# Seven products for one more pair of gate and up blocks, first loads from another queue, and a final norm in two halves

## The chip, the core and the metric

The kernel runs on one core of one Trainium2 chip. The core has TensorE (matmuls into PSUM), VectorE, ScalarE and GpSimd (elementwise work), and SyncE, which issues loads. The time is device time of one execution in microseconds, the median of the runs of a round; it does not include the host.

## The reference, cut to what matters

The model has two layers. Each does a half-weighted SwiGLU feed-forward, a mixer and another half-weighted feed-forward, each behind an RMS norm; the mixer is latent attention in the first layer and a chunked mLSTM in the second. A final RMS norm ends it. There are 512 tokens of width 1024, and the hidden width of a feed-forward is 2816. All is float32.

```python
def rmsnorm(x, g, eps=RMS_EPS):
    xf = x.astype(F32)
    y = xf * lax.rsqrt(jnp.mean(xf * xf, axis=-1, keepdims=True) + eps)
    return (y * g.astype(F32)).astype(x.dtype)

def swiglu(h, w_gate, w_up, w_down):
    return (jax.nn.silu(h @ w_gate) * (h @ w_up)) @ w_down

def reference(...):
    for layer in range(DEPTH):
        x = x + 0.5 * swiglu(rmsnorm(x, ffn_norm[layer, 0]), ...)
        h = rmsnorm(x, mix_norm[layer])
        ...
        x = x + y.astype(x.dtype)
        x = x + 0.5 * swiglu(rmsnorm(x, ffn_norm[layer, 1]), ...)
    return rmsnorm(x, final_norm)
```

## The kernel before

The activations stay in SBUF transposed: eight tiles of 128 features by 512 tokens. There are six phases: f0, a (attention), f1, f2, m (mLSTM), f3. Every float32 operand is split into a high part, rounded by ScalarE (L162, L206), and a low part, the difference, made by VectorE (L163, L207); a product is three matmuls, high by high, high by low, low by high.

A feed-forward has eleven pairs of 128-wide blocks of gate and up. The first NB = 2 pairs are plain (L411): two halves of 48 matmuls of 512 columns each, on inputs with the gain but without the norm's scale, which is applied afterwards. The other nine pairs are groups of seven (L433): gate and up, the two halves of the tokens and the two halves of the features form a 2 x 2 by 2 x 2 block product that is done with seven block products instead of eight, each of 24 matmuls of 256 columns, in the order 1, 6, 5, 7, 2, 3, 4. Their operands need the norm's scale rb beforehand. The statistics come after the first plain half (L423): small matmuls on TensorE (L273), a power on GpSimd (L281), and a spread back over the partitions (L286 to L297). Then normed_blocks (L363) makes the operands in twelve steps: blocks b11, b12, b22, b21 of normed inputs (L373), their differences (L391 to L393, L407) and seven splits. Each step is deferred until a given number of further weight chunks has been asked for (L426).

Weights come in chunks of 128 x 1024 (512 KB). A chunk is split AHEAD = 2 chunks before its use (L186), and the high and the low parts have three buffers each. For a group of seven, five chunks are loaded and two more are added onto loaded ones: the tiles named sum are loaded by SyncE (L122) and get a second block added by an accumulating load from GpSimd (L125), which waits for the first. Two further sums of weights are made by VectorE (L150). SyncE issues loads in order, and a load waits there until its buffer is free: three for raw chunks, and 31 in the arena, which also holds sums, operands and activations.

The first three pairs' results go to the plain part of the down projection; the other eight form two slabs, whose down projection is again done by seven products (L571), the last of them product 4 of four chunks. For the last feed-forward the squares for the final norm are accumulated there (L634 to L641), and finish (L1301) makes the scale of all 512 tokens and multiplies the eight tiles.

In the mLSTM the heads go in pairs (L1223): a pass of the loop makes queries or keys by a convolution (L959), gates, the mixing of two heads with their values (mix), and the decay weights of two heads (decay). In the last pass the first product of the output projection, out(0, 0), stands between decay(6) and the pending sums of squares (L1240 to L1245).

The order of the instructions of an engine is fixed when the program is built: a scheduler takes them by readiness as it expects it and otherwise by the order of the program. On the chip each engine then runs its own list in order.

Of the kernel before, what the change touches and what calls it, by code (L numbers as in the profile page):

```python
# [26 lines left out]
F32 = mybir.dt.float32  # L27
F32R = mybir.dt.float32r
# [3 lines left out]
ALU = mybir.AluOpType  # L32
# [8 lines left out]
H = 8  # L41
W = 1024
NU = NF // 2
NB = 2
DC = 3
ARENA = 31
LOADS = 4
AHEAD = 2
WARM = 36
EPS = 1e-6  # L50
# [14 lines left out]
class Trunk:  # L65
# [48 lines left out]
    def load_pieces(self):  # L114

        name, pieces, pool, plus = self.loads[len(self.loaded)]

        ap = self.row(*name)
        raw = self.duo(pool, F32) if pool else self.wp.tile([P, W], F32, name="raw", tag="raw")
        self.loaded.append(raw)  # L120
        for a, b in pieces:
            self.nc.sync.dma_start(out=raw[:, a:b], in_=ap[:, a:b])  # L122
            yield
        if plus:
            self.nc.gpsimd.dma_start(out=raw, in_=self.row(*plus), accum_op=ALU.add)  # L125
# [105 lines left out]
    def norm_begin(self, gcol):  # L231
        self.xg = [None] * ND
        self.gcol = gcol
        self.acc = self.small.tile([P, T], F32, name="acc", tag="acc", bufs=2)
        self.nacc = 0

    def norm_split(self, d):

# [1 line left out]
        self.split_to(self.xg[d], self.x[d], self.vec(self.gcol + d))  # L240

    def norm_square(self, d):
        self.square(self.acc, self.x[d], self.nacc == 0)
        self.nacc += 1

    def norm_tile(self, d):

# [4 lines left out]
    def norm_half(self, d, n):  # L252

        t = slice(n * T // 2, n * T // 2 + T // 2)
        if self.gcol is not None:
            if self.xg[d] is None:
                self.xg[d] = self.pair()
            self.split_to([a[:, t] for a in self.xg[d]], self.x[d][:, t], self.vec(self.gcol + d))
        self.square(self.acc[:, t], self.x[d][:, t], False)

    def square(self, acc, src, first):
        if first:
# [3 lines left out]
            self.nc.scalar.activation(sq, src, AF.Square)  # L266
            self.nc.vector.tensor_tensor(out=acc, in0=acc, in1=sq, op=ALU.add)

    def rstd(self, acc, n, times=None):

        st = self.ps2.tile([P, T], F32, name="st", tag="st")
        for q in range(NT):
            self.nc.tensor.matmul(st[:, q:q + 1], acc[:, q * P:(q + 1) * P], self.one, start=True, stop=True)  # L273
        ms = self.small.tile([P, NT], F32, name="ms", tag="ms")
        if times is not None:
            self.nc.vector.tensor_tensor(out=ms, in0=st[:, 0:NT], in1=times, op=ALU.mult)
            self.nc.vector.tensor_scalar(ms, ms, 1.0 / n, EPS, ALU.mult, ALU.add)
        else:
            self.nc.vector.tensor_scalar(ms, st[:, 0:NT], 1.0 / n, EPS, ALU.mult, ALU.add)
        r = self.small.tile([P, NT], F32, name="r", tag="r", bufs=6)  # L280
        self.nc.gpsimd.tensor_tensor(out=r, in0=ms, in1=self.mhalf[:, 0:NT], op=ALU.pow)  # L281
        return r

    def spread(self, r):

        hi = self.small.tile([P, NT], F32R, name="rh", tag="rh")  # L286
        lo = self.small.tile([P, NT], F32, name="rl", tag="rl")
        self.split_to((hi, lo), r)
        bc = self.ps2.tile([P, T], F32, name="bc", tag="st")
        for n, part in enumerate((hi.bitcast(F32), lo)):  # L290
            diag = self.tmp.tile([P, T], F32R, name="diag", tag="t")
            self.nc.vector.tensor_tensor(
                out=diag.rearrange("p (a b) -> p a b", a=NT),
                in0=self.ident[:, None, :].broadcast_to([P, NT, P]),
                in1=part[:, :, None].broadcast_to([P, NT, P]), op=ALU.mult)
            self.nc.tensor.matmul(bc, self.onesr, diag, start=n == 0, stop=n == 1)
        return bc  # L297

# [6 lines left out]
    def begin(self, gcol):  # L305
# [10 lines left out]
        for i in range(WARM):  # L316
            nc.tensor.matmul(idle[:, 0:P], warm, warm, start=True, stop=True)
        self.par = self.const.tile([P, V_END], F32, name="par")
        nc.gpsimd.dma_start(out=self.par, in_=self.t["vecs"])
        cst = self.const.tile([P, self.t["cst"].shape[1]], F32, name="cst")  # L320
        nc.gpsimd.dma_start(out=cst, in_=self.t["cst"])
        self.ident = cst[:, 0:P]
# [88 lines left out]
    def plain(self, f, j, half, xg, outs):  # L411

        nc = self.nc
        g, u = self.bank("g"), self.bank("u")
        for k0 in range(0, ND, 4):
            w = self.weights("wgc", f, j, half, k0 // 4)
            for k in range(4):
                for b, o in ((g, 0), (u, P)):
                    self.mm3(b, w(k * 256 + o), xg[k0 + k], k0 + k == 0, k0 + k == ND - 1)
        if j + half == 0:  # L420
            if f == 0:
                self.constants()
            _, self.rb = self.stats()  # L423
            steps = self.normed_blocks(self.rb)
            for i in range(12):
                self.defer(1 + i // 2, lambda: next(steps))  # L426
        gr, ur = self.t512("gr"), self.t512("ur")
        nc.vector.tensor_tensor(out=gr, in0=g, in1=self.rb, op=ALU.mult)
        nc.vector.tensor_tensor(out=ur, in0=u, in1=self.rb, op=ALU.mult)
        nc.scalar.activation(gr, gr, AF.Silu)  # L430
        nc.vector.tensor_tensor(out=outs, in0=gr, in1=ur, op=ALU.mult)
# [139 lines left out]
    def down_seven(self, slabs):  # L571
# [57 lines left out]
        for c in range(4):  # L629
            product(bw, 7, c, last=False)  # L630
            product(bx, 2, c)
        add(1, 1, bw, -0.5)
        add(0, 0, bx, 0.5)
        for d in range(4):  # L634
            self.norm_tile(d)
        for c in range(4):
            product(bw, 4, c, first=False)
            self.norm_half(4 + c, 1)
        add(1, 0, bw, -0.5)
        for d in range(4, 8):  # L640
            self.norm_half(d, 0)  # L641

    def plan_ffn(self, f):
        for j in range(NB):
# [302 lines left out]
    def mlstm(self, next_gain):  # L947
# [258 lines left out]
        def out(part, i):  # L1206
            self.mix_out("wo2", part, i, ys)
# [15 lines left out]
        for p in range(3):  # L1223
            a, b = 2 * p, 2 * p + 1
            conv(p + 5)
            gate(a + 2)
            pending = [mix(a), mix(b)]
            if p == 1:
                steps = factors(0, pending)
                for i in (1, 2, 4):  # L1230
                    self.defer(i, lambda: next(steps))
                values(1)
                for i in range(4):
                    gated(i)
# [75 lines left out]
    def run(self, phases):  # L1310
        gains = {"f0": V_FFN, "f1": V_FFN + ND, "f2": V_FFN + 2 * ND, "f3": V_FFN + 3 * ND,
# [12 lines left out]
        for p, q in zip(phases, phases[1:] + ["end"]):  # L1324
# [104 lines left out]
```

## Time and profile before

| | us |
|---|---|
| median of three runs | 1867.44 (1866.93 to 1869.98) |
| profiled execution, its own time | 1857.42 |
| its span, first to last instruction | 1855.7 |
| TensorE busy | 1811.5 (98%) |
| VectorE busy | 1463.2 (79%) |
| ScalarE busy | 934.9 (50%) |
| GpSimd busy | 131.3 (7%) |

The profile is of one execution, whose time lies 10.0 us under the median of the timed ones. Its mean granted TensorE clock is 0.992 of full speed. In the views PE is TensorE, DVE is VectorE, ACT is ScalarE, POOL is GpSimd, SP is SyncE; a q behind a name is the engine's sequencer, which issues. L with a number is a line of the kernel.

### The profile page before, as it was taken

The numbers are of one execution on the slowest core, as the hardware profiler recorded it, in microseconds if no ns is written. First come the engines' busy times: TensorE is split into PE (matmuls) and PEld (weight loads), VectorE is DVE, ScalarE is ACT, GpSimd is POOL, SyncE is SP. The second block draws the span as 40 slices with busy tenths as digits, with TensorE's granted clock in tenths as the row PEclk, the third lists the DMA queues.
The fourth block names the chain that finished last, engine by engine and source line by source line (L and its number), as shares of the span: only waits on it lengthen the run. The fifth ranks groups of instructions, "written<-read, shape, count | busy, mean of one in ns | idle before, by whom it ended". The sixth has DMA issues, their size and how long they took to land.

```text
span 1855.7 us, 30086 instructions
## 1 busy us (share of the span) xinstructions
PE 1811.5 (98%) x12240; PEld 1662.8 (90%) x12240; DVE 1463.2 (79%) x1931; ACT 934.9 (50%) x1339; POOL 131.3 (7%) x154
## 2 busy tenths in 40 slices
PE   9999999999999999999999999999998999999996
PEld 7999989978887999989989999997876779999896
DVE  7877899777767877877796878778877778788875
ACT  5444545567544444544544444455757544445442
POOL 0010011000000010000001000100000000100010
PEclk9999999999999999999999999999998999999998
DMA  6683567421124684566377456733221246845662
GB/s 205 177 236 110 162 187 163 137 74 63 46 73 150 159 243 128 140 181 153 126 219 205 133 162 187 175 105 101 80 69 57 69 126 181 236 125 149 184 159 91
DMA packets 74906, 265.66 MB, mean 143 GB/s; under 512 B 8336, under 2 KB 9360, under 8 KB 74768
## 3 DMA queue, kind: packets, MB, share of 16 engines
q1 hardware_dynamic: 57312, 200.30, 30.9%
q0 software_dynamic: 17456, 63.44, 19.4%
q8 instruction: 96, 1.57, 0.3%
q14 instruction: 42, 0.34, 0.1%
HBM read 261.62 MB, written 2.10 MB: 142 GB/s over the span
## 4 chain that ended last, share of the span: by engine, by line
PE 73%; issue 13%; DVE 8%; ACT 3%; DMA 2%; POOL 0%; POOLq 0%; DVEq 0%; ACTq 0%
PE pz L450 4%; PE pw L449 4%; PE pw L448 4%; PE pz L449 4%; PE pz L448 4%; PE pw L450 3%; PE y L194 3%; PE y L196 3%; PE y L195 3%; PE px L449 3%; PE px L448 3%; PE px L450 3%; PE py L450 2%; DMA raw<-in_wgs 2%; PE py L448 2%
## 5 line engine op out<-in xcount | busy, mean ns | idle before, releaser
L162 ACT CAST whi<-raw 128x1024 fp32r<-128x1024 f32 (+1 forms) x278 | 284.9, 1025 | 412.2 <-issue 131.1
L163 DVE TENSOR_TENSOR wlo<-raw,whi 128x1024 fp32r<-128x1024 f32 (+1 forms) x278 | 330.5, 1190 | 109.1 <-ACT whi L162 108.1
L162 ACT CAST whi<-sum 128x1024 fp32r<-128x1024 f32 x208 | 217.5, 1047 | 278.5 <-PE pz L449 80.8
L163 DVE TENSOR_TENSOR wlo<-sum,whi 128x1024 fp32r<-128x1024 f32 x208 | 252.8, 1221 | 72.0 <-ACT whi L162 72.0
L150 DVE TENSOR_TENSOR sum<-raw,sum 128x1024 f32<-128x1024 f32 x88 | 107.2, 1219 | 25.6 <-DMA raw<-in_wgs 25.1
L125 POOL DMA_DIRECT2D sum<-in_wgs x72 | 61.6, 855 | 640.2 <-DMA sum<-in_wgs 278.3
L450 PE MATMUL py<-b6h,wlo 128*128 128x256 f32 x288 | 83.5, 290 | 10.6 <-DVE wlo L163 10.5
L448 PE MATMUL py<-b6h,whi 128*128 128x256 f32 x288 | 82.8, 288 | 2.2 <-ACT whi L162 2.2
L449 PE MATMUL py<-b6l,whi 128*128 128x256 f32 x288 | 82.4, 286 | 0.0
L450 PE MATMUL pz<-b5h,wlo 128*128 128x256 f32 x288 | 81.5, 283 | 0.8 <-DVE wlo L163 0.8
L450 PE MATMUL pw<-b7h,wlo 128*128 128x256 f32 x288 | 81.2, 282 | 0.0
L450 PE MATMUL px<-b2h,wlo 128*128 128x256 f32 x288 | 81.2, 282 | 0.0
L450 PE MATMUL pz<-b3h,wlo 128*128 128x256 f32 x288 | 81.2, 282 | 0.0
L450 PE MATMUL pw<-b4h,wlo 128*128 128x256 f32 x288 | 81.2, 282 | 0.0
L449 PE MATMUL pw<-b7l,whi 128*128 128x256 f32 x288 | 81.2, 282 | 0.0
L449 PE MATMUL pz<-b3l,whi 128*128 128x256 f32 x288 | 81.2, 282 | 0.0
L449 PE MATMUL px<-b2l,whi 128*128 128x256 f32 x288 | 81.2, 282 | 0.0
L449 PE MATMUL pw<-b4l,whi 128*128 128x256 f32 x288 | 81.2, 282 | 0.0
L450 PE MATMUL px<-b1h,wlo 128*128 128x256 f32 x288 | 81.2, 282 | 0.0
L449 PE MATMUL px<-b1l,whi 128*128 128x256 f32 x288 | 81.2, 282 | 0.0
L449 PE MATMUL pz<-b5l,whi 128*128 128x256 f32 x288 | 81.2, 282 | 0.0
L448 PE MATMUL px<-b1h,whi 128*128 128x256 f32 x288 | 81.2, 282 | 0.0
(418 smaller groups left out, 6137.1 us busy)
## 6 DMA issues: line engine op xcount, KB each, us to landing
raw<-in_wgs SPq DMA_DIRECT2D x108, 512.0 KB, 4.7
sum<-in_wgs SPq DMA_DIRECT2D x72, 512.0 KB, 6.8
sum<-in_wgs POOLq DMA_DIRECT2D x72, 512.0 KB, 7.2
sum<-in_wds POOLq DMA_DIRECT2D x48, 512.0 KB, 6.0
raw<-in_wds SPq DMA_DIRECT2D x48, 512.0 KB, 3.3
sum<-in_wds SPq DMA_DIRECT2D x32, 512.0 KB, 4.5
raw<-in_wgc SPq DMA_DIRECT2D x30, 512.0 KB, 3.3
raw<-in_wdn SPq DMA_DIRECT2D x24, 512.0 KB, 4.0
```

What stands on the lines that cost most here:

```text
L125: self.nc.gpsimd.dma_start(out=raw, in_=self.row(*plus), accum_op=ALU.add)
L150: self.nc.vector.tensor_tensor(out=t, in0=a, in1=b, op=ALU.add)
L162: self.nc.scalar.copy(out=hi[:, a:b], in_=raw[:, a:b])
L163: self.nc.vector.tensor_tensor(out=lo[:, a:b], in0=raw[:, a:b], in1=hi[:, a:b].bitcast(F32), op=ALU.subtract)
L194: mm(out, lhs[0], rhs[0], start=start, stop=False)
L195: mm(out, lhs[0], rhs[1], start=False, stop=False)
L196: mm(out, lhs[1], rhs[0], start=False, stop=stop)
L448: mm(out, wh, bh[:, b], start=first and e + k == 0, stop=False, skip_group_check=True)
L449: mm(out, wh, bl[:, b], start=False, stop=False, skip_group_check=True)
L450: mm(out, wl, bh[:, b], start=False, stop=last and e + k == 4, skip_group_check=True)
```

## The change

NB becomes 1, so that a feed-forward has one plain pair and ten groups of seven. The twelve steps of normed_blocks get a list of their own, STEPS, of due times. The first load of a tile sum for gate and up goes to GpSimd's queue instead of SyncE's, ahead of the accumulating one. The load of the parameters at the start goes to SyncE's queue instead. In the mLSTM's last pass out(0, 0) is called before decay(6). The final norm is done for tokens 256 to 511 while product 4 of the last down projection is still to come, and for tokens 0 to 255 after it; for the second of these the squares of four tiles are summed by the statistics matmuls instead of VectorE, and the outputs are made by ScalarE with GpSimd for all eight tiles of the first half and for two of the other, and by VectorE for six.

```diff
@@ -41,10 +41,12 @@
 H = 8
 W = 1024
 NU = NF // 2
-NB = 2
+NB = 1
 DC = 3
 ARENA = 31
 LOADS = 4
+
+STEPS = 1, 1, 1, 1, 2, 2, 3, 4, 5, 5, 6, 7
 AHEAD = 2
 WARM = 36
 EPS = 1e-6
@@ -119,7 +121,8 @@
         raw = self.duo(pool, F32) if pool else self.wp.tile([P, W], F32, name="raw", tag="raw")
         self.loaded.append(raw)
         for a, b in pieces:
-            self.nc.sync.dma_start(out=raw[:, a:b], in_=ap[:, a:b])
+            queue = self.nc.gpsimd if plus and name[0] == "wgs" else self.nc.sync
+            queue.dma_start(out=raw[:, a:b], in_=ap[:, a:b])
             yield
         if plus:
             self.nc.gpsimd.dma_start(out=raw, in_=self.row(*plus), accum_op=ALU.add)
@@ -232,7 +235,7 @@
         self.xg = [None] * ND
         self.gcol = gcol
         self.acc = self.small.tile([P, T], F32, name="acc", tag="acc", bufs=2)
-        self.nacc = 0
+        self.nacc = [0, 0]
 
     def norm_split(self, d):
 
@@ -240,8 +243,8 @@
         self.split_to(self.xg[d], self.x[d], self.vec(self.gcol + d))
 
     def norm_square(self, d):
-        self.square(self.acc, self.x[d], self.nacc == 0)
-        self.nacc += 1
+        self.square(self.acc, self.x[d], self.nacc == [0, 0])
+        self.nacc = [n + 1 for n in self.nacc]
 
     def norm_tile(self, d):
 
@@ -256,7 +259,8 @@
             if self.xg[d] is None:
                 self.xg[d] = self.pair()
             self.split_to([a[:, t] for a in self.xg[d]], self.x[d][:, t], self.vec(self.gcol + d))
-        self.square(self.acc[:, t], self.x[d][:, t], False)
+        self.square(self.acc[:, t], self.x[d][:, t], self.nacc[n] == 0)
+        self.nacc[n] += 1
 
     def square(self, acc, src, first):
         if first:
@@ -266,33 +270,38 @@
-    def rstd(self, acc, n, times=None):
+    def rstd(self, acc, n, times=None, tiles=range(NT)):
...
+        accs = acc if isinstance(acc, list) else [acc]
+        for i, q in enumerate(tiles):
+            for k, a in enumerate(accs):
+                self.nc.tensor.matmul(st[:, i:i + 1], a[:, q * P:(q + 1) * P], self.one, start=k == 0,
+                                      stop=k == len(accs) - 1)
...
@@ -316,7 +325,7 @@
         for i in range(WARM):
             nc.tensor.matmul(idle[:, 0:P], warm, warm, start=True, stop=True)
         self.par = self.const.tile([P, V_END], F32, name="par")
-        nc.gpsimd.dma_start(out=self.par, in_=self.t["vecs"])
+        nc.sync.dma_start(out=self.par, in_=self.t["vecs"])
         cst = self.const.tile([P, self.t["cst"].shape[1]], F32, name="cst")
         nc.gpsimd.dma_start(out=cst, in_=self.t["cst"])
         self.ident = cst[:, 0:P]
@@ -422,8 +431,8 @@
                 self.constants()
             _, self.rb = self.stats()
             steps = self.normed_blocks(self.rb)
-            for i in range(12):
-                self.defer(1 + i // 2, lambda: next(steps))
+            for i in STEPS:
+                self.defer(i, lambda: next(steps))
         gr, ur = self.t512("gr"), self.t512("ur")
         nc.vector.tensor_tensor(out=gr, in0=g, in1=self.rb, op=ALU.mult)
         nc.vector.tensor_tensor(out=ur, in0=u, in1=self.rb, op=ALU.mult)
@@ -630,15 +639,23 @@
             product(bw, 7, c, last=False)
             product(bx, 2, c)
         add(1, 1, bw, -0.5)
+        if self.gcol is None:
+            for d in range(8):
+                self.norm_half(d, 1)
+            self.finish(1)
         add(0, 0, bx, 0.5)
         for d in range(4):
-            self.norm_tile(d)
+            self.norm_half(d, 0) if self.gcol is None else self.norm_tile(d)
         for c in range(4):
             product(bw, 4, c, first=False)
-            self.norm_half(4 + c, 1)
+            if self.gcol is not None:
+                self.norm_half(4 + c, 1)
         add(1, 0, bw, -0.5)
-        for d in range(4, 8):
-            self.norm_half(d, 0)
+        if self.gcol is None:
+            self.finish(0)
+        else:
+            for d in range(4, 8):
+                self.norm_half(d, 0)
 
     def plan_ffn(self, f):
         for j in range(NB):
@@ -1237,9 +1254,12 @@
             if p == 0:
                 for f in pending:
                     f()
+            if p == 2:
+                out(0, 0)
             decay(a + 2)
-            conv(p + 2) if p < 2 else out(0, 0)
-            if p == 2:
+            if p < 2:
+                conv(p + 2)
+            else:
                 for f in pending:
                     f()
             decay(b + 2)
@@ -1298,14 +1318,29 @@
             self.plan(("wo2", i // 4, i % 4))
 
 
-    def finish(self):
+    def finish(self, n):
+
+
         nc = self.nc
-        rb = self.spread(self.rstd(self.acc, D))
+        t = slice(n * T // 2, n * T // 2 + T // 2)
+        accs = [self.acc]
+        if n == 0:
+            for d in range(4, 8):
+                accs.append(self.t512("sq"))
+                nc.scalar.activation(accs[-1][:, t], self.x[d][:, t], AF.Square)
+        bc = self.spread(self.rstd(accs, D, tiles=range(2 * n, 2 * n + 2)))
+        rb = self.small.tile([P, T], F32, name="rb", tag="rb", bufs=2)[:, :T // 2]
+        nc.scalar.copy(out=rb, in_=bc)
         for d in range(ND):
-            o = self.t512("o")
-            nc.vector.scalar_tensor_tensor(out=o, in0=self.x[d], scalar=self.vec(V_FIN + d), in1=rb,
-                                           op0=ALU.mult, op1=ALU.mult)
-            nc.sync.dma_start(out=self.out[d * P:(d + 1) * P, :], in_=o)
+            o = self.t512("o")[:, :T // 2]
+            gain = self.vec(V_FIN + d)
+            if n or d % 3 == 2:
+                nc.scalar.activation(o, self.x[d][:, t], AF.Identity, scale=gain)
+                nc.gpsimd.tensor_tensor(out=o, in0=o, in1=rb, op=ALU.mult)
+            else:
+                nc.vector.scalar_tensor_tensor(out=o, in0=self.x[d][:, t], scalar=gain, in1=bc,
+                                               op0=ALU.mult, op1=ALU.mult)
+            nc.sync.dma_start(out=self.out[d * P:(d + 1) * P, t], in_=o)
 
     def run(self, phases):
         gains = {"f0": V_FFN, "f1": V_FFN + ND, "f2": V_FFN + 2 * ND, "f3": V_FFN + 3 * ND,
@@ -1328,7 +1363,6 @@
                 self.mla(gains[q])
             else:
                 self.mlstm(gains[q])
-        self.finish()
```

## Rows read from the trace of the kernel before

**Rows 1.** The page, part 1: busy time of each engine (share of the span).

```profile
PE 1811.5 (98%) x12240; PEld 1662.8 (90%) x12240; DVE 1463.2 (79%) x1931; ACT 934.9 (50%) x1339; POOL 131.3 (7%) x154
```

**Rows 2.** Waits of PE, whole span: total us, times, longest us.

```profile
PE py L450 <- DVE wlo L163: 10.5, 7, 2.5
```

**Rows 3.** Timeline of PE in f1: start us, us, engine, line, what [idle before].

```profile
582.28 0.39 PE L194 MATMUL g<-pr,whi 128*128 128x512 f32 x1
...
604.68 0.28 PE L448 MATMUL px<-b1h,whi 128*128 128x256 f32 x1
...
626.41 0.28 PE L448 MATMUL px<-b1h,whi 128*128 128x256 f32 x1
...
646.57 0.28 PE L448 MATMUL px<-b1h,whi 128*128 128x256 f32 x1
```

**Rows 4.** Timelines of DVE and PE in f0, plain pairs and first group.

```profile
27.87 0.68 DVE L428 TENSOR_TENSOR gr<-g,rb 128x512 f32<-128x512 f32 x1
...
32.12 0.39 PE L194 MATMUL g<-pr,whi 128*128 128x512 f32 x1
...
54.52 0.28 PE L448 MATMUL px<-b1h,whi 128*128 128x256 f32 x1
...
77.57 0.28 PE L448 MATMUL px<-b1h,whi 128*128 128x256 f32 x1
```

**Rows 5.** Timelines of PE, DVE and SP around the fourth group of f0.

```profile
117.89 0.28 PE L448 MATMUL px<-b1h,whi 128*128 128x256 f32 x1
...
142.15 0.28 PE L448 MATMUL px<-b1h,whi 128*128 128x256 f32 x1
...
120.61 1.23 DVE L150 TENSOR_TENSOR sum<-raw,sum 128x1024 f32<-128x1024 f32 x1 [5.72 <-DMA raw<-in_wgs]
...
74.92 16.92 SPq L122 DMA_DIRECT2D raw<-in_wgs  x3
...
111.67 3.25 SPq L122 DMA_DIRECT2D raw<-in_wgs  x2
```

**Rows 6.** mLSTM: timeline of PE, and one window (us, busy..., PEclk, DMA share, GB/s).

```profile
1418.31 0.27 PE L196 MATMUL num<-pr 128*128 128x128 f32 x1
...
1425.78 0.77 PE L200 MATMUL s<-qz,pr 128*128 128x512 f32 x1 [3.72 <-DVE pr L737]
...
1428.15 0.73 PE L194 MATMUL y<-pr,whi 128*128 128x512 f32 x1
...
1420.44:1430.68 10.24, 5.70 (x15) 4.54 (x16) 7.83 (x12) 9.17 (x15) 0.00 (x0) 0.50 0.30 103
```

**Rows 7.** Timelines of PE, POOL and DVE behind the last product.

```profile
1841.84 1.02 PE L273 MATMUL st<-cst,acc 128*128 128x1 f32 x8 [2.79 <-DVE acc L267]
...
1843.15 1.03 POOL L281 TENSOR_TENSOR r<-ms,mhalf 128x4 f32<-128x4 f32 x1 [52.50 <-DVE ms L279]
...
1845.35 1.31 PE L296 MATMUL bc<-diag,onesr 128*128 128x512 f32 x2 [2.48 <-DVE diag L292]
...
1846.70 5.36 DVE L1306 SCALAR_TENSOR_TENSOR o<-xx,par,bc 128x512 f32<-128x512 f32 x8 [0.89 <-PE bc L296]
```

**Rows 8.** Timeline of DVE in f1, from the plain pairs on.

```profile
575.17 0.69 DVE L428 TENSOR_TENSOR gr<-g,rb 128x512 f32<-128x512 f32 x1 [1.21 <-ACT rb L301]
...
577.72 1.67 DVE L373 SCALAR_TENSOR_TENSOR xn<-xx,par,rb 128x256 f32<-128x256 f32 x4
...
603.31 1.22 DVE L207 TENSOR_TENSOR b3l<-xn,b3h 128x1024 fp32r<-128x1024 f32 x1
604.44 1.22 DVE L207 TENSOR_TENSOR b4l<-xn,b4h 128x1024 fp32r<-128x1024 f32 x1
```

**Rows 9.** The page, parts 5 (mean ns of one) and 6 (us to landing).

```profile
L125 POOL DMA_DIRECT2D sum<-in_wgs x72 | 61.6, 855 | 640.2 <-DMA sum<-in_wgs 278.3
...
sum<-in_wgs SPq DMA_DIRECT2D x72, 512.0 KB, 6.8
```

**Rows 10.** Timeline of ACT at the start.

```profile
5.38 0.72 ACT L209 ACTIVATE pr<-xx,par 128x512 fp32r<-128x512 f32 x1 [3.16 <-DMA par<-in_vecs]
```

More of the change, by code (lines that the diff above doesn't have):

```diff
@@ L267, in square @@
             self.nc.vector.tensor_tensor(out=acc, in0=acc, in1=sq, op=ALU.add)
-    def rstd(self, acc, n, times=None):
+    def rstd(self, acc, n, times=None, tiles=range(NT)):
         st = self.ps2.tile([P, T], F32, name="st", tag="st")
-        for q in range(NT):
-            self.nc.tensor.matmul(st[:, q:q + 1], acc[:, q * P:(q + 1) * P], self.one, start=True, stop=True)
-        ms = self.small.tile([P, NT], F32, name="ms", tag="ms")
+        m = len(tiles)
+        accs = acc if isinstance(acc, list) else [acc]
[3 more added lines that the diff above has]
+                                      stop=k == len(accs) - 1)
+        ms = self.small.tile([P, NT], F32, name="ms", tag="ms")[:, :m]
@@ L275, in rstd @@
         if times is not None:
-            self.nc.vector.tensor_tensor(out=ms, in0=st[:, 0:NT], in1=times, op=ALU.mult)
+            self.nc.vector.tensor_tensor(out=ms, in0=st[:, 0:m], in1=times, op=ALU.mult)
             self.nc.vector.tensor_scalar(ms, ms, 1.0 / n, EPS, ALU.mult, ALU.add)
         else:
-            self.nc.vector.tensor_scalar(ms, st[:, 0:NT], 1.0 / n, EPS, ALU.mult, ALU.add)
-        r = self.small.tile([P, NT], F32, name="r", tag="r", bufs=6)
-        self.nc.gpsimd.tensor_tensor(out=r, in0=ms, in1=self.mhalf[:, 0:NT], op=ALU.pow)
+            self.nc.vector.tensor_scalar(ms, st[:, 0:m], 1.0 / n, EPS, ALU.mult, ALU.add)
@@ L282, in rstd @@
+        r = self.small.tile([P, NT], F32, name="r", tag="r", bufs=6)[:, :m]
+        self.nc.gpsimd.tensor_tensor(out=r, in0=ms, in1=self.mhalf[:, 0:m], op=ALU.pow)
         return r
     def spread(self, r):
-        hi = self.small.tile([P, NT], F32R, name="rh", tag="rh")
-        lo = self.small.tile([P, NT], F32, name="rl", tag="rl")
+        m = r.shape[1]
+        hi = self.small.tile([P, NT], F32R, name="rh", tag="rh")[:, :m]
+        lo = self.small.tile([P, NT], F32, name="rl", tag="rl")[:, :m]
@@ L288, in spread @@
         self.split_to((hi, lo), r)
-        bc = self.ps2.tile([P, T], F32, name="bc", tag="st")
+        bc = self.ps2.tile([P, T], F32, name="bc", tag="st")[:, :m * P]
         for n, part in enumerate((hi.bitcast(F32), lo)):
-            diag = self.tmp.tile([P, T], F32R, name="diag", tag="t")
+            diag = self.tmp.tile([P, T], F32R, name="diag", tag="t")[:, :m * P]
             self.nc.vector.tensor_tensor(
-                out=diag.rearrange("p (a b) -> p a b", a=NT),
-                in0=self.ident[:, None, :].broadcast_to([P, NT, P]),
-                in1=part[:, :, None].broadcast_to([P, NT, P]), op=ALU.mult)
+                out=diag.rearrange("p (a b) -> p a b", a=m),
+                in0=self.ident[:, None, :].broadcast_to([P, m, P]),
+                in1=part[:, :, None].broadcast_to([P, m, P]), op=ALU.mult)
```

## The prediction

> **What bounds the kernel now.** I read the page first, then the waits of TensorE, then its timeline, and last the timelines of VectorE, SyncE and ScalarE around each place where TensorE stood still. TensorE is busy 98% of the span [rows 1], and what it waits for longest is the low part of the weights, 10.5 us in 7 waits [rows 2]. Busy overstates its work, since a matmul's record is longer than its turn, so I went by starts: in the seven-product groups a 256-column matmul starts every 0.12 us and a group of 168 lasts 626.41 to 646.57, that is 20.16 us or 2.88 us a product [rows 3]. Twenty-eight of the 36 groups have this length to within 0.02 us, the other eight are the first and the fourth of each FFN; elsewhere in the groups VectorE, ScalarE, GpSimd and the loads are hidden. So a change gains only by fewer matmuls or by shorter halts of TensorE, and loses by new halts.
>
> The halts, by starts. The first group of an FFN takes 77.57 - 54.52 = 23.05 us in f0, 2.89 over 20.16 [rows 4]; in f1 it is 626.41 - 604.68 = 21.73, 1.57 over [rows 3]; f2 and f3 read in the same way give 0.36 and 1.56. Together 6.4. The fourth group takes 142.15 - 117.89 = 24.26 in f0, 4.10 over [rows 5]; f1, f2 and f3 are 4.08, 2.61 and 2.66 over. Together 13.4. The mLSTM has one hole of some 7 us [rows 6], and after the last product 16 us are a serial tail [rows 7].
>
> **Products.** The second plain pair of f1, 96 matmuls of 512 columns, lasts from 582.28 to 604.68 [rows 3], 22.40 us without a halt, 0.233 each. A group of 20.16 in its place saves 2.24, four times: -9.0. This is certain as far as TensorE stays fed.
>
> **The passage from plain to seven.** This is the main cost. The scale rb, which all operands need, is ready in f1 at 575.13, just before VectorE's first product with it [rows 8]. Before, TensorE has 29.5 us of plain work from there (to 604.68); after, one pair ends where the second began, at 582.28 [rows 3], and only 7.1 us are left. VectorE is what fills the time: before, it runs from 575 to beyond 605 almost without a break. I add what VectorE must have done before the last product of the first group (product 4, after six of 2.88 us, so without halts at 582.28 + 17.28 = 599.6). Four blocks of four pieces: a row of four takes 1.67 and the next starts after 1.6, so 6.4. Four sums or differences of blocks, seven splits of operands, six splits of weights and one sum of weights, each 1.13 (604.44 - 603.31) [rows 8]: 18 x 1.13 = 20.4. Two products with rb, which free two PSUM banks, 1.2. Together 28.0, so 603.2: a halt of 3.6 at least. Everything else that stands before it in the program (three instructions for the activations of one half and one of the other, four combinations of 0.6 each, two of 0.34, one more sum) is 6.6, which gives 609.8 and a halt of 10.2. The scheduler orders by readiness, so part of it slips behind: I take the middle, 6.9, for f1, f2 and f3 alike, since in each rb comes 7 us before the second pair's first matmul. In f0 rb comes at 27.8 and the pair ends at 32.12 [rows 4], and VectorE is too full before to make the second product's sum of weights ahead: 27.87 + 29.1 = 57.0 to 63.0 against 32.12 + 17.28 = 49.4, a halt of 7.6 to 13.6, middle 10.6. All four: 3 x 6.9 + 10.6 = 31.3 (18.4 to 44.2). The 6.4 of today are in this place and go: +24.9 net (+12.0 to +37.8). The new STEPS do what can be done: they put the operands of product 1 and 6 first and spread the rest over the group.
>
> **First loads on GpSimd.** In the fourth group VectorE stood 5.72 us behind one sum of weights that waited for a load [rows 5], which the scheduler had put far ahead of its need; the lows of the next product queued behind it, and TensorE halted. That load, issued at 111.67, took 8.9 us to land. It was one of a crowd: SyncE's queue had stood within a row of three loads from 74.92 for 16.92 us, waiting for a buffer of raw weights, with first loads of the sums queued behind [rows 5], and then issued them close together. With the first loads on GpSimd that queue no longer holds them. The cost on GpSimd is 80 issues of 0.86 each [rows 9], hidden: GpSimd is busy 7% [rows 1]. But each accumulating load waits on GpSimd's own queue until its first load landed, and now the next first load, and in the plain stage the power that makes rb, are queued behind that wait. Per group two waits of some 6.8 us [rows 9] plus four issues are 17 us of the 20.16, so it fits, without much room. I take -8 (0 to -13.4).
>
> **Output product earlier in the mLSTM.** Between 1418.31 and 1425.78 TensorE starts two matmuls of rows and waits, 3.72 us of it for the split keys; the clock is granted at half (1.2 GHz) from 1420.44 to 1430.68, and the 24 matmuls of out(0, 0), 24 x 0.233 = 5.6 us at full clock, begin behind the hole at 1428.15 [rows 6]. out(0, 0) needs nothing of that wait; moved ahead of decay it fills 5.6 of the 7.5 us, and at full clock. Then ScalarE and VectorE, which do the next decay, end the chain. I take -5 (-3, if they bound it, to -7).
>
> **The tail.** Today: eight statistics matmuls, 1.02 after a wait of 2.79; the power 1.03; two spreading matmuls 1.31; eight outputs of 512 columns, 5.36 [rows 7]. After, the last half has no four additions (-1.1) but twelve small matmuls behind the last square instead of eight (+0.5), half-size diagonals and spreading (-1.0), and six outputs of 256 columns on VectorE, 2.4 instead of 5.36 (-2.9); two go by ScalarE and GpSimd beside them. That is -4.5. The first half's statistics cost TensorE about 1 us within product 4, and TensorE halts there if the power is late. No row has a multiplication on GpSimd; VectorE's piece of 256 columns (0.4) [rows 8] and the power on four columns (1.03) are the nearest, so eight of them are 3 to 8 us of the 11.5 that product 4 lasts: hidden, or at the upper end just ahead of the last power. I take 0.7 each and -3.5 (-5 to 0). The Trainium skill ("GPSIMD Engine Reference", Elementwise) gives 2.6 cycles an element for two inputs, an estimated 0.55 us and its dispatch; by it the sum stays.
>
> **Start.** The first activation waits 3.16 us for the parameters [rows 10]. On SyncE's queue they come earlier but push every load of x by one issue, 0.4 us: 0 (-1 to +2).
>
> **Sum.** -9.0 + 24.9 - 8 - 5 - 3.5 + 0 = -0.6. The profiled execution took 1857.42 (span 1855.7), so 1856.8; its time lies 10.0 below the median 1867.44 of the timed runs, and I apply the difference to that: 1866.8. What a measurement here can tell from no change is 0.2%, 3.7 us.
>
> **Rivals.** First, VectorE's order is near the strict list, the halts 4.5 three times and 8.5: net +15.6, the rest as above, -9.9: 1857.5. For it: TensorE's order already skips matmuls that are not ready. Against it: today's order leaves VectorE idle for some tenths at a time even there. Second, the fourth-group halts go wholly and the mLSTM gains 7: -8.0, 1859.4. For it: all four halts have one cause. Third, slower: the queue move gains nothing, because GpSimd's queue now holds the first loads behind its accumulating ones as SyncE's did behind raw ones, so that the crowd of loads stays; term 0 instead of -8: +7.4, 1874.8. It decides once the wait for one first load exceeds about 8.5 us, when a group's loads no longer fit in 20.16. Beside it stands the Trainium skill ("Trainium Kernel Development and Optimization", Key Constraints): the queues of SyncE, ScalarE and GpSimd share the same 16 DMA engines, and issuing from several saves only issue time; by that rule too the term is 0. The row of 16.92 us speaks against it, since there the order of one queue and no engine held the loads. Fourth, slower: VectorE follows the program's order nearly wholly, the halts 9.5 three times and 13: net +35.1, the sum +9.6, 1877.0.
>
> **How the numbers follow.** The forecast, within 3.7 us of before, has 0.30; first rival 0.22, second 0.16, third 0.16, fourth 0.16. Faster by over 0.2%: 0.38; within: 0.30; slower: 0.32. First and fourth rival with their neighbours of both signs reach 1852 and 1880; outside I leave 0.2. The forecast's own range is 1863 to 1871.
>
> **What would show it.** Right: ten groups an FFN of 20.16; halts in the first group of 6 to 8 us in f1 to f3 and more in f0, ended by VectorE's low parts of operands; no wait of a sum of weights on a raw load in the later groups; y matmuls between num and s in the mLSTM; outputs ending 3 to 4 us sooner behind the last product. Wrong: first groups within 3 us of 20.16 (then VectorE had slack that I don't see), rb later than 7 us before the end of an FFN's plain pair because the power stood behind a load on GpSimd, or halts that moved to other groups.

## The result, and the profile after

The changed kernel takes 1900.28 us (median of four runs, 1899.26 to 1902.37) against 1867.18 for the kernel before, a ratio of 1.0179 (95% interval 1.0160 to 1.0198): 33 us slower, outside the forecast range. Its profiled execution took 1902.37 us, its span 1900.6 against 1855.7. The spans differ by 44.9 us and the medians by 33.1, since the profiled execution of the kernel before lies 9.8 under its median and that of the changed one 2.1 above.

The page of the changed kernel: part 1 (busy us, share of the span, instructions) and one group of part 5 (busy, mean ns | idle before, releaser).

```profile
PE 1821.9 (96%) x12546; PEld 1686.5 (89%) x12546; DVE 1484.8 (78%) x1964; ACT 954.7 (50%) x1379; POOL 192.7 (10%) x252
...
L457 PE MATMUL py<-b6h,whi 128*128 128x256 f32 x320 | 94.8, 296 | 34.9 <-ACT whi L165 34.9
```

The waits of TensorE (total us, times, longest us), where [rows 2] had 10.5 us as its first line:

```profile
PE py L457 <- ACT whi L165: 34.9, 4, 9.4
PE px L457 <- ACT b1h L209: 6.0, 1, 6.0
PE py L459 <- DVE wlo L166: 5.4, 7, 1.4
PE g L197 <- ACT whi L165: 3.6, 3, 2.5
...
PE s L203 <- DVE pr L754: 2.6, 1, 2.6
...
PE ab L1026 <- DVE a L1202: 1.5, 1, 1.5
```

Four waits hold 34.9 us, one for each feed-forward, all before product 6 of the first group. TensorE's timeline of f1, which answers to [rows 3], shows one of them (start us, us, engine, line, what, [idle before]):

```profile
604.37 0.28 PE L457 MATMUL px<-b1h,whi 128*128 128x256 f32 x1
...
616.84 0.58 PE L457 MATMUL py<-b6h,whi 128*128 128x256 f32 x1 [9.44 <-ACT whi L165]
...
636.25 0.39 PE L458 MATMUL pw<-b4l,whi 128*128 128x256 f32 x1
```

Product 1 starts on time, product 6 comes 9.4 us late, and product 4, which would begin at 604.37 + 17.28 = 621.65 without halts, gets its low part at 636.2: this matmul starts 0.05 us behind the end of VectorE's record of b4l, and so it is in all four feed-forwards. VectorE's timeline in the same stretch, which answers to [rows 8]:

```profile
597.26 0.69 DVE L437 TENSOR_TENSOR gr<-g,rb 128x512 f32<-128x512 f32 x1 [1.21 <-ACT rb L310]
...
599.20 0.69 DVE L440 TENSOR_TENSOR act<-gr,ur 128x512 f32<-128x512 f32 x1 [0.66 <-ACT gr L439]
...
602.60 1.23 DVE L210 TENSOR_TENSOR b1l<-xn,b1h 128x1024 fp32r<-128x1024 f32 x1 [1.12 <-ACT b1h L209]
...
613.30 1.22 DVE L210 TENSOR_TENSOR b6l<-xn,b6h 128x1024 fp32r<-128x1024 f32 x1 [1.11 <-ACT b6h L209]
614.44 1.22 DVE L153 TENSOR_TENSOR sum<-raw,sum 128x1024 f32<-128x1024 f32 x1
...
624.22 0.69 DVE L471 TENSOR_TENSOR u<-u,py 128x512 f32<-128x512 f32 x1 [1.30 <-PE py L459]
...
634.97 1.23 DVE L210 TENSOR_TENSOR b4l<-xn,b4h 128x1024 fp32r<-128x1024 f32 x1 [0.50 <-ACT b4h L209]
```

From rb at 597.26 to the end of product 4's low part at 634.97 + 1.14 = 636.1 are 38.9 us, of which 34.2 are work and 4.7 are the five waits in brackets behind the first row. One of the five, 1.30, is for TensorE's own product 6. TensorE covers 621.65 - 597.26 = 24.4 of it. What is left, 14.5, is how late product 4 gets its operand; by starts the first group is 14.3 us too long. Of these, 10.1 are halts in products 6 and 5, and the rest is lost in 8.1 us of matmuls at half clock behind them.

Where the 44.9 us of span went, read by the starts of TensorE's products in both traces (first group: it and what slips of it into the second):

| part | forecast | measured |
|---|---|---|
| products, ten groups for one pair | -9.0 | -9.0 |
| passage: first groups 15.0, 14.3, 12.5, 14.0 over, and f0's wait for b1h 6.2, less 6.4 | +24.9 | +55.6 |
| fifth and sixth groups (the same pairs of blocks as the fourth and fifth before): 8.3 over, less 13.4 | -8 | -5.1 |
| start and f0's plain pair | 0 | +5.5 |
| mLSTM (f2's down projection with it) | -5 | -3.1 |
| f3's down projection and the tail | -3.5 | -0.6 |
| attention, with the down projections of f0 and f1 | 0 | +1.5 |

### The profile page after: what moved, and what is told of

The parts are those of the page before. It is cut to its first block, busy times and chain, and to the rows that moved or that the text cites. A ratio compares the mean times of both kernels' runs of the same rounds, so it can differ in the third digit from the quotient of the medians.

```text
span 1900.6 us, 30783 instructions
## 1 busy us (share of the span) xinstructions
PE 1821.9 (96%) x12546; PEld 1686.5 (89%) x12546; DVE 1484.8 (78%) x1964; ACT 954.7 (50%) x1379; POOL 192.7 (10%) x252
## 4 chain that ended last, share of the span: by engine, by line
PE 69%; issue 12%; DVE 7%; DMA 6%; ACT 3%; POOL 1%; SPq 0%; DVEq 0%; POOLq 0%; ACTq 0%
PE pz L459 4%; PE pw L458 4%; PE pw L457 4%; PE pw L459 4%; PE pz L458 4%; PE pz L457 4%; PE px L459 3%; PE px L458 3%; PE px L457 3%; PE y L197 3%; PE y L198 3%; PE y L199 2%; DMA raw<-in_wgs 2%; DMA sum<-in_wgs 2%; PE py L459 2%
## 5 line engine op out<-in xcount | busy, mean ns | idle before, releaser
L165 ACT CAST whi<-raw 128x1024 fp32r<-128x1024 f32 (+2 forms) x274 | 280.8, 1025 | 411.9 <-issue 127.0
L166 DVE TENSOR_TENSOR wlo<-raw,whi 128x1024 fp32r<-128x1024 f32 (+2 forms) x274 | 325.6, 1190 | 108.7 <-ACT whi L165 108.0
L165 ACT CAST whi<-sum 128x1024 fp32r<-128x1024 f32 x224 | 233.1, 1047 | 272.2 <-PE pz L458 70.3
L166 DVE TENSOR_TENSOR wlo<-sum,whi 128x1024 fp32r<-128x1024 f32 x224 | 271.4, 1220 | 73.1 <-ACT whi L165 73.0
L457 PE MATMUL py<-b6h,whi 128*128 128x256 f32 x320 | 94.8, 296 | 34.9 <-ACT whi L165 34.9
L125 POOL DMA_DIRECT2D sum<-in_wgs x80 | 50.4, 646 | 494.8 <-DVE wlo L166 386.2
L459 PE MATMUL py<-b6h,wlo 128*128 128x256 f32 x320 | 95.2, 298 | 5.4 <-DVE wlo L166 5.4
L128 POOL DMA_DIRECT2D sum<-in_wgs x80 | 69.5, 869 | 283.1 <-DMA sum<-in_wgs 243.3
L457 PEld LDWEIGHTS py<-b6h,whi 128*128 128x128 f32 x320 | 64.4, 201 | 35.7 <-ACT whi L165 35.7
L458 PE MATMUL py<-b6l,whi 128*128 128x256 f32 x320 | 94.0, 294 | 0.0
L457 PE MATMUL pz<-b5h,whi 128*128 128x256 f32 x320 | 91.8, 287 | 0.6 <-ACT whi L165 0.5
```

The source lines that it names most:

```text
L125: queue.dma_start(out=raw[:, a:b], in_=ap[:, a:b])
L165: self.nc.scalar.copy(out=hi[:, a:b], in_=raw[:, a:b])
L166: self.nc.vector.tensor_tensor(out=lo[:, a:b], in0=raw[:, a:b], in1=hi[:, a:b].bitcast(F32), op=ALU.subtract)
L457: mm(out, wh, bh[:, b], start=first and e + k == 0, stop=False, skip_group_check=True)
L458: mm(out, wh, bl[:, b], start=False, stop=False, skip_group_check=True)
L459: mm(out, wl, bh[:, b], start=False, stop=last and e + k == 4, skip_group_check=True)
```

## Experiments

Two theories stood after this. V: the passage is the length of VectorE's list from rb to the last operand. Q: it is the first loads, which the changed queue puts behind the power on GpSimd (in f1 the power starts at 592.45 and a first load is issued right behind it, at 594.40). A third cause could be the clock: it is granted at half (1.2 GHz) from 611.3 to 625.0 in f1, from within the halt on, and TensorE works at half speed for 8 us of that.

**The queue undone.** All first loads on SyncE's queue again.

```diff
-            queue = self.nc.gpsimd if plus and name[0] == "wgs" else self.nc.sync
+            queue = self.nc.sync
```

> The changed kernel with the first loads of the gate and up sums issued by SyncE again; everything else of the change stays. Theory V (the halt at product 6 of each first group is the length of VectorE's list between rb and the sum of weights, and the queue matters only for f0's start): the halts of 9.0 to 9.6 us before py6 in f1, f2 and f3 stay within 1 us; f0's first matmul of gate and up loses its waits of 2.65 and 1.12 us and f0's plain stage ends about 5 us sooner; the fourth and fifth groups get back some 5 us of halts in all (13.4 before the change, 8.3 after). Net about 0 to -3: 1897 to 1900. Theory Q (the late first loads set the halt at product 6): py6's halts fall by 3 us or more in each of f1 to f3, and f0's passage by 8: 1885 to 1890.

**The queue undone for first groups alone.**

```diff
-            queue = self.nc.gpsimd if plus and name[0] == "wgs" else self.nc.sync
+            queue = self.nc.gpsimd if plus and name[0] == "wgs" and name[2] else self.nc.sync
```

> The changed kernel with the first loads of the first group of each feed-forward on SyncE's queue, those of the other nine groups on GpSimd's. Theory V: the halts before py6 in f1 to f3 stay within 1 us of 9.0 to 9.6, f0's plain stage ends about 5 us sooner and the wait for b1h there with it, the later groups stay as after the change: 1893 to 1896. Theory Q: the halts before py6 fall by 3 us or more each, f0's passage by 8: 1880 to 1884.

Measured: 1901.57 (ratio to before 1.0203, 1.0188 to 1.0218) and 1898.45 (1.0189, 1.0174 to 1.0204), 1.6 and 2.5 us above what V gave. f0's wait for b1h, which V let go in the second, stayed at 6.0. TensorE's timeline of f1 in the second of these kernels, and VectorE's sum of weights for product 6:

```profile
608.49 0.58 PE L457 MATMUL py<-b6h,whi 128*128 128x256 f32 x1 [9.44 <-ACT whi L165]
...
606.08 1.22 DVE L153 TENSOR_TENSOR sum<-raw,sum 128x1024 f32<-128x1024 f32 x1
```

The halt is the same 9.44 us to the hundredth, although here the loads of that sum had landed by 582.0, 24 us before VectorE came to it. Q falls: the sum stands behind b6l in VectorE's list and not behind a load. The changed kernel's own trace says so too: the load at 594.40 is for the second group, and the two sums of the first, issued at 525.35 and 530.38, were complete at 542.0, 72 us before VectorE came to them at 614.44.

What the queue does cost is f0's plain pair. With all first loads on SyncE it takes 24.3 us instead of 30.5, with the rest as in the changed kernel. GpSimd and ScalarE at the start of the changed kernel:

```profile
2.39 1.07 POOL L125 DMA_DIRECT2D sum<-in_wgs  x2
9.03 0.90 POOL L128 DMA_DIRECT2D sum<-in_wgs  x1 [5.56 <-DMA sum<-in_wgs]
...
18.28 0.72 ACT L212 ACTIVATE pr<-xx,par 128x512 fp32r<-128x512 f32 x1 [2.48 <-DMA xx<-in_xT]
```

Here the loads of two sums (1 MB), and behind them their accumulating loads from 9.03 on, run beside the inputs, whose last one lands at 20.82; with SyncE it lands at 12.73. And the queue does help the later groups: their excess is 11.9 us with SyncE, 7.3 with GpSimd for all but the first group. The two effects nearly cancel in the total.

**Two plain pairs again, everything else changed.**

```diff
-NB = 1
+NB = 2
-STEPS = 1, 1, 1, 1, 2, 2, 3, 4, 5, 5, 6, 7
+STEPS = 1, 1, 2, 2, 3, 3, 4, 4, 5, 5, 6, 6
```

> The changed kernel with two plain pairs and nine groups of seven again, and the twelve steps at their old due times (two per chunk); queue, mLSTM order and final norm stay changed. If the tenth group is the whole cause of the slowdown (the passage costs about 57 us and saves 9 us of products), the time falls by 44 to 50: 1852 to 1858 by the median, with first groups at most 3 us over 20.16. Rival: the queue move itself delays the operands and the start, so that the first groups stay 5 us or more over and f0's start stays 5 us late: 1872 to 1880.

Measured: 1857.32 (ratio 0.9968, 0.9955 to 0.9981), 43 us below the changed kernel (39 by the ratios to before). Its first groups are 4.4, 3.5, 0.4 and 2.0 us over 20.16, two of them more than the 3 that were expected. So the tenth group is the cause: about 52 us of halts for 9 of products. The run puts the due times back too; what they do by themselves was not run.

**The halt filled.** Seventy matmuls that nobody reads, behind product 1.

```diff
+        if fill:
+            idle = self.ps2.tile([P, T], F32, name="idle", tag="st")
+            for i in range(fill):
+                mm(idle[:, 0:HT], self.onesr, self.ops[1][0][:, 0:HT], start=True, stop=True)
...
-                self.seven(outs)
+                self.seven(outs, 70 if j == NB else 0)
```

> The changed kernel with 70 matmuls of 256 columns that nobody reads, 65 of them between product 1 and product 6 of each first group (8.4 us at 0.12 each), in the place where TensorE halts. If the half clock behind the halts (13.65, 13.65, 10.24 and 13.65 us long, about 30 us of it with work) costs time of its own, the granted clock stays at 1.0 there, products 6 and 5 last 2.9 instead of up to 4.9, and the first groups shorten by 2.5 to 4 us each: 1886 to 1890. Rival: VectorE's list is what sets the end of the group, and at full clock TensorE only halts again further on, for the low parts of later operands: within 2 us of 1900.

Measured: 1905.40 (ratio 1.0231, 1.0205 to 1.0257). One window, first of the changed kernel and then of this one (us, busy us of PE, PEld, DVE, ACT, POOL with counts, PEclk, DMA share, GB/s), and two rows of this one's TensorE:

```profile
616.84:624.98 8.14, 7.46 (x31) 6.87 (x32) 6.84 (x10) 2.82 (x4) 0.56 (x1) 0.50 1.02 291
```

```profile
616.84:624.98 8.14, 6.87 (x55) 6.57 (x55) 8.12 (x12) 4.30 (x5) 0.56 (x1) 1.00 0.80 193
```

```profile
607.05 8.09 PE L473 MATMUL idle<-b1h,onesr 128*128 128x256 f32 x68
616.43 0.39 PE L457 MATMUL py<-b6h,whi 128*128 128x256 f32 x1 [1.28 <-ACT whi L165]
...
631.30 0.39 PE L459 MATMUL pz<-b3h,wlo 128*128 128x256 f32 x1 [1.06 <-DVE wlo L166]
```

In f1 the clock stays at full, and TensorE, now faster, halts again at product 3 for a low part. The passages of f0, f1 and f2 are 1.6, 1.5 and 0.3 us shorter than in the changed kernel. In f3 the clock fell to half all the same, for 6.8 us from 1565.7 on, and its passage is 1.5 longer; the four together are 1.9 shorter. The total is not, as the later groups have 3.4 us more halts: the profiled execution is 1.5 us longer, the median 5.1, and the traces don't show where the rest is. So the half clock costs little here, at most 1.6 us of a passage: it spends time in which VectorE is late anyway.

**VectorE's list, in three doses.** All three start from the kernel with the first groups on SyncE's queue (1898.45). First, rb sooner: the statistics, and the deferral of the twelve steps with them, are called after half of the first half's matmuls.

```diff
             for k in range(4):
                 for b, o in ((g, 0), (u, P)):
                     self.mm3(b, w(k * 256 + o), xg[k0 + k], k0 + k == 0, k0 + k == ND - 1)
-        if j + half == 0:
+            if j + half + k0 == 0:
...
```

> The kernel of the run e3_first_group_syncq with one thing moved: the statistics and the deferral of the twelve operand steps are called after the first 24 matmuls of the plain pair instead of after the first 48. In f1 the squares are summed at 584.0 and TensorE took the statistics matmuls only at 592.1; so rb can come 5.6 us earlier in f1, f2 and f3, in f0 0 to 3 us earlier, because the inputs land later there. If the passage is the length of VectorE's list from rb to the low part of product 4's operand (38.9 us against 24.4 that TensorE can cover), each first group shortens by as much: 1898.4 - 17 to 20 = 1878 to 1882. Rival: loads, the queue or the clock set it: within 3 us of 1898.

Second, 1.8 us less in the list: the three VectorE instructions (and one of ScalarE) that finish the second half are deferred by seven chunks, behind product 4's low part.

```diff
...
+        if half:
+            self.defer(7, activate)
+        else:
+            activate()
```

> The kernel of the run e3_first_group_syncq with the three VectorE instructions that finish the second half of the plain pair (0.6 us each, 1.8 together) moved behind the operands of the first group. If VectorE's list sets the passage, the halt before py6 and the first group shorten by 1.8 us in each feed-forward, in f0 too: 1898.4 - 7 = 1891. Rival: VectorE has slack there and something else ends the halts: within 2 us of 1898.

Third, 3.4 us more: three low parts are made twice.

```diff
+        for p, b in ((6, b11), (5, b12), (7, t3)):
+            v.tensor_tensor(out=ops[p][1], in0=b, in1=ops[p][0].bitcast(F32), op=ALU.subtract)
```

> The kernel of the run e3_first_group_syncq with three VectorE instructions done twice in each first group (the low parts of the operands of products 6, 5 and 7, 1.13 us each, with the same result). If VectorE's list sets the end of the first group, each of the four lengthens by 3.4 us: 1898.4 + 13.6 = 1912. Rival: VectorE idles for 4.7 us in the passage, behind ScalarE's copies and behind TensorE, and takes the added work in there: 1898 to 1901.

Measured: 1877.82 (ratio 1.0091, 1.0075 to 1.0107), 1892.74 (1.0168, 1.0152 to 1.0184) and 1914.92 (1.0284, 1.0266 to 1.0303): -20.6, -5.7 and +16.5 by the medians where -17 to -20, -7 and +13.6 were expected. The base was timed in an earlier round; by the ratios to before of each round they are -18, -4 and +18. The traces say it more closely. With early statistics the first groups of f1 to f3 (with what slips into the second) are 7.2, 4.8 and 6.5 us shorter. f0 is 1.0 longer up to the end of its second group: the spread of rb still stands behind the whole plain pair there, and rb comes no sooner. Without the three instructions f1 to f3 give 2.1, 1.5 and 2.4; f0 nothing. With three more, the four groups take 4.3, 3.8, 3.7 and 2.7 more. In f1 the time from rb to the end of product 4's low part was 37.7 + 1.1 = 38.8 in the base, 36.8 with the late activations and 42.6 with the doubled low parts. VectorE in f1, in the base, with the late activations and with the doubled low parts:

```profile
588.90 0.69 DVE L437 TENSOR_TENSOR gr<-g,rb 128x512 f32<-128x512 f32 x1 [1.21 <-ACT rb L310]
...
626.59 1.22 DVE L210 TENSOR_TENSOR b4l<-xn,b4h 128x1024 fp32r<-128x1024 f32 x1 [0.47 <-ACT b4h L209]
```

```profile
588.81 0.69 DVE L439 TENSOR_TENSOR gr<-g,rb 128x512 f32<-128x512 f32 x1 [1.21 <-ACT rb L310]
...
624.44 1.23 DVE L210 TENSOR_TENSOR b4l<-xn,b4h 128x1024 fp32r<-128x1024 f32 x1
```

```profile
596.14 0.69 DVE L439 TENSOR_TENSOR gr<-g,rb 128x512 f32<-128x512 f32 x1 [1.21 <-ACT rb L310]
...
637.62 1.23 DVE L210 TENSOR_TENSOR b4l<-xn,b4h 128x1024 fp32r<-128x1024 f32 x1
```

The kernel with early statistics, VectorE and TensorE in f1:

```profile
581.34 1.67 DVE L382 SCALAR_TENSOR_TENSOR xn<-xx,par,rb 128x256 f32<-128x256 f32 x4 [1.22 <-ACT rb L310]
...
610.94 1.22 DVE L210 TENSOR_TENSOR b4l<-xn,b4h 128x1024 fp32r<-128x1024 f32 x1
...
594.05 0.28 PE L457 MATMUL px<-b1h,whi 128*128 128x256 f32 x1
...
600.30 0.38 PE L457 MATMUL py<-b6h,whi 128*128 128x256 f32 x1 [3.22 <-ACT whi L165]
```

rb is there 12.7 us before product 1 instead of 7.1, and the halt before product 6 is 3.22 instead of 9.44. This dose is not rb alone: the steps also fall due one chunk sooner, so that VectorE's list has another order. Product 4's low part is done 30.7 us after rb, 6.5 before TensorE comes to it, and what is left of the halt belongs to product 6. The third dose has a flaw: product 6 waits for its own doubled low part (8.4 us in four waits), so TensorE meets part of the added work directly. V rests above all on the second dose, which only takes work away; the other two agree with it.

**The parts that leave gate and up alone.** The kernel before with the mLSTM order and the final norm of the change.

> The kernel before with the two parts of the change that do not touch gate and up: out(0, 0) ahead of decay(6) in the mLSTM, and the final norm in halves. By the traces of before and after, the time from the second down projection of the first mixer's layer to f3 fell by 3.1 us, and the time behind the last product by 1.9 with 0.7 lost to a halt in product 4. So 4.3 us less than before: ratio 0.9977, faster in the mLSTM by 3 and in the tail by 1. Rival: the hole of the mLSTM only moves to the wait of ab (1.5 us) and the tail gains nothing: ratio 0.999 to 1.0.

Measured: ratio 0.9983 (0.9970 to 0.9995), some 3 us; the interval takes in the forecast and a part of the rival's range. The stretch of the mLSTM is 4.6 us shorter than in the trace of before, the time from the last product to the end 14.3 instead of 16.9.

**A better kernel.** Two plain pairs, the changed queue, mLSTM and norm, and the statistics early; the second with the first groups' first loads on SyncE's queue.

> The kernel of the run e2_two_pairs (two plain pairs, changed queue, mLSTM order and final norm) with the statistics called after the first 24 matmuls of the plain pair. Its first groups were 4.4, 3.5, 0.4 and 2.0 us over 20.16. If VectorE's list from rb on sets these too, rb 5.6 us earlier takes them away in f1 to f3 (5.9 in all) and up to 4.4 in f0: 1857.3 - 6 to 10 = 1847 to 1851, ratio to before 0.992 to 0.994. Rival: with two pairs these halts are late loads of GpSimd's queue: ratio 0.997 as without the early statistics.

> The kernel of the run b1_two_pairs_early with the first loads of each feed-forward's first group on SyncE's queue. If what is left in its first groups is a load late on GpSimd's queue behind the power, this kernel is 2 to 5 us faster than b1; if it is VectorE's list alone, the two agree within 2 us.

Measured: 1849.54 (ratio 0.9926, 0.9911 to 0.9942) and 1848.31 (0.9919, 0.9902 to 0.9936), against 1864.92 for the kernel before in their round. In both, the first groups of f1 to f3 have 20.16 us, and f0's has 22.6. Both are faster than the kernel before and the changed one; between them there is no difference that these runs can tell.

## Why the prediction was wrong

**Products.** Right: the tenth group saves 2.24 us, and six of the ten groups of each feed-forward have 20.16.

**The passage: the step that failed.** rb came 7.1 us before the pair's end in f1, as worked out, and the list was counted right: 28.0 strict plus 6.6 other is 34.6, and the trace has 34.2. Two things made 6.9 out of what is 14.5. I took the middle between the strict and the full list, because "the scheduler orders by readiness, so part of it slips behind". Nothing slipped behind: the activations of both halves, the combinations and the second sum all stand ahead of b4l in the profile. The three activations of the second half even stand among the differences for product 6, which the program puts before them. And I counted work without waits: each split is a copy on ScalarE and then a subtraction on VectorE, and where the next instruction of the list needs that low part, VectorE stands 1.1 us. With the others, one of them for TensorE itself, that is 4.7. So the halt is the upper bound's 10.2, less 0.4 for the list, plus 4.7: 14.5. The fourth rival named the right mechanism and gave 1877; it missed the same 4.7 us per feed-forward. The result lies beyond all rivals; the chances of forecast and rivals add up to 1.00, so the 0.2 left for outside had no room. In f0 the upper end 63.0 is not the sum of its terms (27.87 + 29.1 + 6.6 = 63.6), which decides nothing.

The place was wrong too. I set the whole list against the last product and expected the halt there. TensorE stops at the second product, which needs three blocks, three differences, its own split behind product 1's and a sum of weights, with the activations of both halves between them: 18.4 us of the list from rb on, and 1.2 until ScalarE has copied the sum's high part, for 7.1 + 2.9 us of cover. STEPS puts these first, but they are half of the list.

In f0 there is one more step that I did not have. There TensorE's list holds the spread of rb behind the whole plain pair [rows 4: before, rb came within it]:

```profile
32.74 0.68 DVE L301 TENSOR_TENSOR diag<-cst,rl 128x512 fp32r<-128x512 f32 x1
38.49 0.69 DVE L437 TENSOR_TENSOR gr<-g,rb 128x512 f32<-128x512 f32 x1 [5.07 <-ACT rb L310]
...
43.83 0.58 PE L457 MATMUL px<-b1h,whi 128*128 128x256 f32 x1 [6.00 <-ACT b1h L209]
```

The diagonals are ready at 33.4, the spread runs at 37.2, and product 1 waits 6.0 us for its operand. That moving the spread would give these 3.8 us back was not tried.

**First loads on GpSimd.** Half right. The fourth group's halt, in the fifth group now, has shrunk and not gone:

```profile
140.15 1.22 DVE L153 TENSOR_TENSOR sum<-raw,sum 128x1024 f32<-128x1024 f32 x1 [3.72 <-DMA raw<-in_wgs]
```

It is the same wait as in [rows 5], 3.72 instead of 5.72. The load behind it is still issued late (133.21), after 9.9 us in which SyncE waits for a buffer of the arena. The kernel before had the same wait, SyncE's queue from 70 to 120 us:

```profile
SPq L122 <- DVE slab L455: 26.5, 3, 16.0
```

The longest, 16.0, is the 16.92 of [rows 5], which the prediction read as a wait for a buffer of raw weights, and 7.6 of the others end with the issue at 111.67. Both are waits for a buffer of the arena, ended by a VectorE instruction that writes a group's result (slab), and in the changed kernel that wait is still there. The load only lands sooner, in 6.9 us instead of 8.9; with six loads in all under way in its time instead of eight, crowding is the likely reason, but no run shows it by itself. The third rival, no gain at all, was too pessimistic for the groups, but right for the total, by luck: the loss came in a place that no step had, f0's plain pair, 6.2 us, and with the queue undone the time is the same within the intervals. The Trainium skill ("Trainium Kernel Development and Optimization", Key Constraints) has the queues share the same 16 DMA engines. In f0's start the trace agrees: with SyncE alone the engines are busy 98% from 2.0 to 12.7 us, so the loads moved to a free queue there took them from the inputs.

**Start.** TensorE's first matmul comes 0.7 us later (7.16 against 6.45), inside the bounds, but not as the step had it. The parameters land at 2.75 instead of 5.36; the wait moves to the constants, still loaded by GpSimd, of which ScalarE now converts four pieces ahead of its first activation. ScalarE, which answers to [rows 10]:

```profile
5.40 0.30 ACT L354 CAST onesr<-cst 128x128 fp32r<-128x128 f32 x1 [3.17 <-DMA cst<-in_cst]
...
6.10 0.72 ACT L212 ACTIVATE pr<-xx,par 128x512 fp32r<-128x512 f32 x1
```

The rest of the 5.5 is the queue, above: its 6.2, less some 1.3 by which the pair without it is shorter than the first pair before.

**mLSTM.** Right in mechanism and nearly in size: -3.1, and -4.6 without the other parts; over the traces of all runs it is -1.6 to -4.6. The wait at s fell from 3.7 [rows 6] to 2.6, the half clock around it lasts 3.4 us instead of 10.2, and a new wait of 1.5 stands further on, at ab, with another 3.4 us of half clock.

**The tail.** Too good. Behind the last product it is 14.7 us instead of 16.9, of which a halt of 0.7 in product 4, for the first half's spread, gives back some. A single trace says little here: the last output lands 12.9 to 14.3 us behind the last product in all eleven kernels with this norm, 15.5 before, but the span ends another 1.0 to 3.9 later, and in six of them it ends as late as before, 16.8 to 17.4. Timelines of PE, GpSimd and DVE, which answer to [rows 7]:

```profile
1886.57 0.35 PE L280 MATMUL st<-cst,acc 128*128 128x1 f32 x2 [0.45 <-DVE acc L271]
1887.57 1.30 PE L280 MATMUL st<-cst,sq 128*128 128x1 f32 x8 [0.65 <-ACT sq L1330]
...
1880.86 6.15 POOL L1339 TENSOR_TENSOR o<-o,rb 128x256 f32<-128x256 f32 x8 [2.10 <-ACT rb L1333]
...
1893.13 2.44 DVE L1341 SCALAR_TENSOR_TENSOR o<-xx,par,bc 128x256 f32<-128x256 f32 x6 [1.08 <-ACT rb L1333]
```

The small matmuls were miscounted: two token tiles with five sources each are ten matmuls, which the trace shows as twenty records (before, four as eight), instead of the twelve records that I had. With their wait for the squares they last from 1886.57 to 1889.99, 3.4 us instead of 1.02. GpSimd's eight products take 0.77 each, where 0.7 was taken. The Trainium skill ("GPSIMD Engine Reference", Elementwise) has 2.6 cycles an element for two inputs, an estimated 0.55 without dispatch. The trace lies above it. The eight products run until 1887.01, about 1 us behind product 4, and are still hidden, since GpSimd's next work, the last power, starts at 1890.27. VectorE's six took the 2.4 worked out.

## What to carry to other kernels

When a stage that hides another engine's work gets shorter, lay that engine's list out in the order of the program, with the round trips to its neighbours, and set each consumer's deadline against its own prefix of the list, the early ones above all; don't credit reordering that the trace doesn't show. A scale that many operands wait for is worth making as early as its inputs allow: here the same small matmuls a quarter of a pair earlier, with the steps that hang on them, were worth some 18 us in the kernel with ten groups, more than the 9 of products saved. And a load that moves to a free queue at the start competes with the loads that the first matmul needs.

## What the runs showed that was not expected

- A half clock behind a halt cost little: where the clock stayed at full instead (f1's window 616.84 to 624.98, 1.00 instead of 0.50, and in f0 and f2), a passage was 0.3 to 1.6 us shorter, because VectorE was what TensorE waited for.
- GpSimd's power on four columns takes 1.01 to 1.04 us in some places and 1.95 to 1.99 in others, in both kernels (before: 1.04 in f0, 1.96 in f1); in f0 it went from 1.04 to 1.95 with the change. The runs don't show why.
